# Weight pieces split ahead on POOL, and gate projections moved, in a two-block kernel of one core

## The chip, the core and the metric

The kernel runs on one core of a Trainium2 chip. Its engines are named here as the profile names them: PE multiplies matrices (TensorE), DVE, ACT and POOL work on vectors (VectorE, ScalarE, GpSimd), SP (SyncE) issues most of the transfers. The metric is the device time of one execution in microseconds (us), lower is better.

## What is computed

Two blocks follow each other, all in float32, on 512 tokens of width 1024. The first has two layers of mixer, cross-attention and feed-forward, each followed by a layer norm:

```python
for layer in range(2):
    x = layer_norm(alpha * x + mixer(x), ...)
    x = layer_norm(alpha * x + cross_attend(x, mem, ...), ...)
    x = layer_norm(alpha * x + conv_ffn(x, w_up, conv_w, conv_b, w_down), ...)
```

The second modulates the norm of x, projects it with one wide matrix, and runs a recurrent mixer and a banded attention beside each other:

```python
h = rms_norm(x, norm_g) * (1 + scale) + shift
proj = h @ w_in
ps = token_shift(proj[..., :D_SHIFT], mu_shift)      # r, k, v, g, and two low-rank inputs
y_r, g_r = rwkv7_mix(ps, ...)                        # 8 heads of 64, a state per head, token after token
q, ka, va, g_a = split(proj[..., D_SHIFT:], 4)
y_a = chunk_band_attention(q, ka, va, ...)           # 8 heads, a chunk of 64 sees itself and 8 before
y = concat(y_r * silu(g_r), y_a * silu(g_a))
x = x + gate * (y @ w_out)
```

## The kernel before

Activations stand with channels on the 128 partitions and the 512 tokens in the columns. Every large product is done in three: the weights and the activations are split into a high and a low part, and `mm3` (L260 to L265) issues high by high, high by low and low by high. A piece of weights is 128 output channels by 1024 inputs, 512 KB; with 512 tokens it feeds 8 x 3 = 24 products.

`piece` (L239) brings one: SP loads the raw 512 KB, ACT casts it to the high part (L229), and a subtract gives the low part (L230). That subtract runs on DVE in the first block and on POOL in the second (`None if self.extra else self.nc.gpsimd`). The tiles `w` are a ring of four, with two more (`wx`) in the first block, and the raw tiles a ring of two, with one more there.

`ffn` (L619) goes through its hidden channels in three chunks: the up products of a chunk, a gate piece and a value piece in turn, and then its down products, eight pieces. The epilogue of a value piece (`epi`, `m < NF`) multiplies by the gate and splits the hidden tile `hd`; that of a down piece (`epi_d`) adds to the residual x. After the last chunk come the last layer norm of the first block (`ln_half`, L382 to L412), the modulation (L710) and `open2`, which does the second block's first five projections, those of the list `OPEN`, and so r1 among them.

The second block (`block2`, L1285) has one line of work with waits. Four times `rwkv_pair` (L866) prepares two heads of the recurrence: decays and scaled keys on DVE, ACT and POOL, with L894 giving the input of the product `pb` (L834), L905, L914, L915 and L919 on POOL, and L921 a small copy on DVE. Then `rwkv_invert` (L991) inverts the triangular blocks: a chain of 31 steps on DVE (L1003, L1005), a store and a load, transposes (L1027), and two groups of small products (L834) with `fill(FILL[7])` ahead of them and `fill(FILL[8])` behind each. Then `rwkv_chain` goes through the states.

Everything else of the second block is background work, a list of generators in the order of the table ORDER: r are projections of the recurrence, q those of the attention's queries and keys, v its values (four pieces, and two goes through them), g the eight gates, p and a the attention's softmax and output, y the gating, o the last projection. `fill(us)` takes steps from the front of the list until their estimated time is spent, but takes none whose mile (the number ahead of it in ORDER) is above the line's own: 0 to 3 in the pairs, 4 in the inversion, 5 in the state chain. What a step of the line itself needs is pulled out by `need`. A scheduler then orders each engine's instructions by readiness within what the code fixes.

Of the kernel before, what the change touches and what calls it, by code (L numbers as in the profile page):

```python
# [8 lines left out]
F32 = mybir.dt.float32  # L9
# [6 lines left out]
P = 128  # L16
# [23 lines left out]
FILL = (1.12, 3, 1.5, 4, 2.08, 4.16, 23.8, 2.4, 2.4, 0.4, 4)  # L40
# [132 lines left out]
class Prog:  # L173
# [69 lines left out]

    def raw(self):
        self.n += 1
        if self.extra and self.n0 % 3 == 2:
            self.n0 += 1
            return self.t("rawx", [P, 1024], F32, 1)
        self.n0 += 1
        return self.keep.tile([P, 1024], F32, tag="raw", name=f"raw_{self.n}", bufs=2)  # L250

    def wtile(self):
        """The weights' ring: some of its room is there only in the first block."""
# [13 lines left out]
    def lin(self, src, ms, xs, epi, n=S, first=0, last=0):  # L267
        """The first (last) few blocks go through one half of the tokens, then through the other, for the LN
        before (after) them; epi(m, psum, tokens) gets the last ones by halves."""
# [43 lines left out]
    def flush(self):  # L313
        """The LN that is due."""
# [6 lines left out]
    def lin_tm(self, src, pieces, xs, ntok, epi):  # L321
        """out[tok tiles][128, 512 cols]: activations stationary, weights moving."""
# [20 lines left out]
    def rsqrt(self, y, t, v, eps):  # L343
        """y = (v + eps) ** -0.5: the table's value and a Newton step; eps is a column of self.eps."""
# [7 lines left out]
    # residual, then LN over the channels  # L352
# [61 lines left out]
    # mixer of layer 0  # L414
# [204 lines left out]
    def ffn(self, l, xs):  # L619
        nc = self.nc  # L620
        for c, (f0, f1) in enumerate(CHUNKS):
# [3 lines left out]
            def epi(m, ps, ts):  # L625
# [9 lines left out]
                else:  # L635
                    h = self.tmp()
                    nc.vector.tensor_tensor(out=h, in0=ps, in1=keep["g"], op=ALU.mult)
                    hs.append(self.split(self.hd(), h))

# [5 lines left out]
            def epi_d(m, ps, ts):  # L645
# [5 lines left out]
                if c == 1 and l == 0 and m == 1:  # L651
                    self.ada_end()
                if c == 2:
# [6 lines left out]
    # the modulation of the second block, gathered a piece at a time  # L660
# [23 lines left out]
    def ada_end(self):  # L684
        nc = self.nc
        # the sum over the partitions: within 32 of them by turning 32-blocks, then over the four groups
# [18 lines left out]
    def modulate(self, ts):  # L705
        """rms_norm(x) * norm_g * (1 + scale) + shift of half of the tokens."""
# [16 lines left out]
    def open2(self):  # L723
        """The second block's first products, of the first half of the tokens."""
# [48 lines left out]
    # The second block has one line of work with long waits (the states) and much other work for the tensor  # L773
    # engine: `bg` holds the latter as generators, and fill() puts some of it wherever the former waits.
# [57 lines left out]
    def mm(self, out, **kw):  # L832
        """A product on the line with the waits: it stays behind what fill() put before it."""
# [5 lines left out]
    def lin_g(self, src, m, xs, epi, ks=range(KT)):  # L839
        w = self.piece(self.a[src][m])  # L840
# [25 lines left out]
    def rwkv_pair(self, j):  # L866
        """What the chunks of heads 2j and 2j+1 need."""
# [9 lines left out]
        # kk  # L877
# [12 lines left out]
        # k'  # L890
        nc.scalar.activation(u, av, AF.Identity, bias=self.ka1[:, j : j + 1], scale=self.v("k_a_2", j))
        nc.vector.tensor_tensor(out=k, in0=k, in1=u, op=ALU.mult)
        # bonus
# [7 lines left out]
        # decays  # L901
# [20 lines left out]
        # values by token  # L922
# [20 lines left out]
        # scores within the chunks  # L943
# [25 lines left out]
        # keys by token  # L969
# [10 lines left out]
        # the part of the right sides that no state enters  # L980
# [10 lines left out]
    def rwkv_invert(self, prs):  # L991
        """(I - N)^-1 of each chunk's strictly triangular N: 32-blocks by substitution, then the block between."""
# [58 lines left out]
    def rwkv_chain(self, prs, tt):  # L1051
# [40 lines left out]
        def line(i, pr):  # L1092
            for _ in chunks(i, pr):
                yield FILL[9]
            # group norm, then the gate
# [33 lines left out]
    def att_v(self, half, xs):  # L1129
        """Values of two token tiles."""  # L1130
        self.va += [self.t("va", [P, S], F32, 4) for _ in range(2)]
        banks = [self.bank() for _ in range(2)]
        for jj in range(4):
            w = self.piece(self.a["in_va"][jj])
# [12 lines left out]
    def att_epi(self, m, ps):  # L1147
        """Queries or keys of a pair of heads, normed."""
# [15 lines left out]
    def att_probs(self, j):  # L1164
        """Softmax of a pair of heads: a tile holds a chunk's queries of one head, then of the other."""
# [60 lines left out]
    def gate_epi(self, n):  # L1226
        """silu(x) = (tanh(x / 2) + 1) * x / 2; the half comes where it is used."""
# [143 lines left out]
```

## Time and profile before

| | |
|---|---|
| median of three runs | 1854.24 us (1853.18 to 1855.95) |
| span of the profiled execution | 1854.5 us |
| PE busy | 1786.7 us, 96% |
| DVE busy | 1096.3 us, 59% |
| ACT busy | 783.0 us, 42% |
| POOL busy | 362.8 us, 20% |
| HBM read, written | 181.36 MB, 9.18 MB |

The span is that of one execution, taken by the hardware profiler; no time of that execution other than its span is recorded. Busy times of the engines lie beside each other, so they don't add up to the span. A table by stretches says more: the same engine is busy throughout in one stage and waits in another. PEclk in such a table is TensorE's granted clock, 1.0 for 2.4 GHz and 0.5 for 1.2 GHz.

### The profile page before, as it was taken

The page shows a single profiled execution, that of the slowest core. Times are in us where ns is not written, and L with a number is a line of the kernel's source. Part 1 is how long each engine was busy: PE and PEld are TensorE (multiplying, and loading weights), DVE is VectorE, ACT ScalarE, POOL GpSimd, SP SyncE. Part 2 cuts the span into 40 slices and gives each one's busy share as a digit, 9 for nine tenths or more (in the row PEclk, how much of TensorE's full clock was granted, in tenths as well). Part 3 has the DMA queues.
Part 4 walks back from the last instruction along what each step waited for, and adds up shares of the span by engine and source line. Part 5 has one row for each costly group of instructions (what it writes and reads, how often), then busy time and mean ns, then how long its engine had stood idle before and what let it go on. Part 6 is the DMA issues. An engine that isn't in the chain of part 4 may idle for free.

```text
span 1854.5 us, 26344 instructions
## 1 busy us (share of the span) xinstructions
PE 1786.7 (96%) x10476; PEld 1502.4 (81%) x10476; DVE 1096.3 (59%) x1741; ACT 783.0 (42%) x1319; POOL 362.8 (20%) x331
## 2 busy tenths in 40 slices
PE   8999998999999999999999999999998888879999
PEld 7889988888888888988998988888887766656657
DVE  5676689743463467444565764343447666975673
ACT  5444534532332356232453642232335645535561
POOL 0115014000000051000501400000015455623232
PEclk9999999999999999999999999999999999989999
DMA  8431455332322226333131242323222222222142
GB/s 279 145 103 60 132 181 188 100 102 91 102 92 91 80 64 196 112 96 100 59 104 35 69 125 92 102 92 100 88 86 73 82 75 88 89 74 81 56 160 103
DMA packets 62635, 192.25 MB, mean 104 GB/s; under 512 B 7344, under 2 KB 10032, under 8 KB 62512
## 3 DMA queue, kind: packets, MB, share of 16 engines
q1 hardware_dynamic: 54432, 172.25, 29.0%
q0 software_dynamic: 3248, 9.44, 1.5%
q10 hardware_dynamic: 4832, 8.88, 1.4%
q8 instruction: 82, 1.34, 0.3%
q14 instruction: 41, 0.34, 0.1%
HBM read 181.36 MB, written 9.18 MB: 103 GB/s over the span
## 4 chain that ended last, share of the span: by engine, by line
PE 76%; DVE 15%; ACT 3%; issue 3%; DMA 2%; POOL 0%; SPq 0%; DVEq 0%; ACTq 0%; POOLq 0%
PE ch L264 10%; PE ch L263 10%; PE ch L265 10%; PE mm L263 9%; PE mm L265 9%; PE mm L264 9%; PE pv L264 3%; PE pv L263 3%; PE pv L265 3%; PE ch L834 3%; DVE x L401 2%; DVE xh L405 1%; DVE w L230 1%; DVE x L400 1%; DVE vt L681 1%
## 5 line engine op out<-in xcount | busy, mean ns | idle before, releaser
L263 PE MATMUL mm<-xh,w 128*128 128x512 f32 (+1 forms) x704 | 266.1, 378 | 8.5 <-ACT w L229 7.5
L265 PE MATMUL mm<-xh,w 128*128 128x512 f32 (+1 forms) x704 | 258.6, 367 | 0.8 <-DVE w L230 0.8
L264 PE MATMUL mm<-xh,w 128*128 128x512 f32 (+1 forms) x704 | 259.0, 368 | 0.0
L370 POOL TENSOR_TENSOR t<-x,x 128x512 f32<-128x512 f32 x6 | 8.1, 1351 | 1011.1 <-ACT w L229 656.1
L229 ACT CAST w<-raw 128x1024 fp32r<-128x1024 f32 (+2 forms) x131 | 133.1, 1017 | 164.0 <-PE ch L265 62.9
L263 PEld LDWEIGHTS mm<-xh,w 128*128 128x128 f32 x704 | 135.6, 193 | 35.7 <-ACT w L229 7.8
L264 PE MATMUL ch<-xh,w 128*128 128x512 f32 (+1 forms) x432 | 154.1, 357 | 0.6 <-DVE xh L405 0.5
L264 PEld LDWEIGHTS mm<-xh,w 128*128 128x128 f32 x704 | 135.9, 193 | 22.9 <-issue 3.4
L263 PE MATMUL ch<-xh,w 128*128 128x512 f32 (+1 forms) x432 | 153.0, 354 | 1.3 <-ACT xh L404 1.3
L265 PE MATMUL ch<-xh,w 128*128 128x512 f32 (+1 forms) x432 | 152.7, 353 | 1.5 <-DVE w L230 1.5
L265 PEld LDWEIGHTS mm<-xh,w 128*128 128x128 f32 x704 | 135.8, 193 | 22.6 <-issue 1.1
L229 ACT CAST wx<-raw 128x1024 fp32r<-128x1024 f32 (+1 forms) x85 | 88.1, 1039 | 152.4 <-PE ch L265 71.5
L230 DVE TENSOR_TENSOR w<-rawx,w 128x1024 fp32r<-128x1024 f32 (+2 forms) x85 | 104.1, 1225 | 68.0 <-ACT w L229 67.6
L229 ACT CAST w<-rawx 128x1024 fp32r<-128x1024 f32 (+2 forms) x85 | 87.3, 1027 | 116.4 <-PE mm L265 71.0
L230 DVE TENSOR_TENSOR w<-raw,w 128x1024 fp32r<-128x1024 f32 (+2 forms) x90 | 113.0, 1257 | 37.8 <-ACT w L229 37.4
L230 DVE TENSOR_TENSOR wx<-raw,wx 128x1024 fp32r<-128x1024 f32 (+1 forms) x85 | 107.6, 1267 | 27.6 <-ACT wx L229 27.4
L230 POOL TENSOR_TENSOR w<-raw,w 128x1024 fp32r<-128x1024 f32 x41 | 100.4, 2456 | 119.0 <-ACT w L229 115.1
L263 PE MATMUL ch<-xh,wx 128*128 128x512 f32 (+1 forms) x304 | 103.5, 341 | 0.0
L265 PE MATMUL ch<-xh,wx 128*128 128x512 f32 (+1 forms) x304 | 103.0, 339 | 0.0
L264 PE MATMUL ch<-xh,wx 128*128 128x512 f32 (+1 forms) x304 | 103.0, 339 | 0.0
L263 PE MATMUL mm<-hd,w 128*128 128x256 f32 (+1 forms) x304 | 97.7, 322 | 3.6 <-ACT hd L229 3.6
L265 PE MATMUL mm<-hd,w 128*128 128x256 f32 (+1 forms) x304 | 97.9, 322 | 0.0
(484 smaller groups left out, 4498.6 us busy)
## 6 DMA issues: line engine op xcount, KB each, us to landing
raw<-in_up SPq DMA_DIRECT2D x56, 512.0 KB, 3.5
rawx<-in_up SPq DMA_DIRECT2D x32, 512.0 KB, 3.5
kt<-in_ada SPq DMA_DIRECT2D x48, 256.0 KB, 3.3
raw<-in_dn SPq DMA_DIRECT2D x24, 512.0 KB, 3.5
raw<-in_in_r SPq DMA_DIRECT2D x24, 512.0 KB, 3.5
raw<-in_c_in SPq DMA_DIRECT2D x16, 512.0 KB, 3.5
raw<-in_xo SPq DMA_DIRECT2D x12, 512.0 KB, 3.6
raw<-in_xv SPq DMA_DIRECT2D x11, 512.0 KB, 4.1
```

Source lines behind the costliest of these rows:

```text
L229: nc.scalar.copy(hi, src)
L230: (eng or nc.vector).tensor_tensor(out=lo, in0=src, in1=f32(hi), op=ALU.subtract)
L263: mm(out, lhsT=ah, rhs=bh, start=start, stop=False)
L264: mm(out, lhsT=ah, rhs=bl, start=False, stop=False)
L265: mm(out, lhsT=al, rhs=bh, start=False, stop=stop)
L370: eng.tensor_tensor(out=sz, in0=self.x[0][:, ts] if m == 1 else sz, in1=z, op=ALU.add)
L400: (nc.vector if k in DVE_SUB else nc.gpsimd).tensor_tensor(out=x, in0=x, in1=mn, op=ALU.subtract)
L401: nc.vector.scalar_tensor_tensor(out=x, in0=x, scalar=gk, in1=rs, op0=ALU.mult, op1=ALU.mult)
L405: nc.vector.scalar_tensor_tensor(out=lo, in0=x, scalar=bk, in1=f32(hi), op0=ALU.add, op1=ALU.subtract)
L681: nc.vector.scalar_tensor_tensor(out=dst, in0=raw, scalar=sc, in1=dst, op0=ALU.mult, op1=ALU.add)
L834: self.tc.keep_in_program_order(self.nc.tensor.matmul(out, **kw))
```

## The change

The table ORDER loses r1, and the gates g1 and g2 go from mile 5 to mile 4, behind g0. FILL[7] goes from 2.4 to 9 and FILL[8] from 2.4 to 4.2.

In the feed-forward stage of layer 1, `pre_begin` makes a list of 28 pieces of the second block (r, q, g and the four of v that ORDER names) and `pre_step` is called with each value piece of the up products and with each piece of the first two chunks' down products. A step starts the load of one piece through POOL's queue, after a copy of one element of the tile that has just been made; once two are under way, POOL casts and subtracts the older one and stores both parts, 1 MB, to DRAM. The tiles for it, `vt`, are two.

In the second block `ready` takes the place of `piece`: if a piece has been split ahead, SP loads its 1 MB straight into the ring `w`, and nothing is cast or subtracted. The eight pieces of w_out are still split there. The other lines of the diff take comments away.

```diff
-FILL = (1.12, 3, 1.5, 4, 2.08, 4.16, 23.8, 2.4, 2.4, 0.4, 4)
+FILL = (1.12, 3, 1.5, 4, 2.08, 4.16, 23.8, 9, 4.2, 0.4, 4)
...
-    (0, "r1"), (0, "r5"), (0, "r9"),
+    (0, "r5"), (0, "r9"),
...
-    (4, "v1"), (4, "q18"), (4, "q22"), (4, "q19"), (4, "q23"), (4, "g0"),
-    (5, "p0"), (5, "g1"), (5, "q20+a0"), (5, "p1"), (5, "q24+a1+p2"), (5, "g2"), (5, "g3"),
+    (4, "v1"), (4, "q18"), (4, "q22"), (4, "q19"), (4, "q23"), (4, "g0"), (4, "g1"), (4, "g2"),
+    (5, "p0"), (5, "q20+a0"), (5, "p1"), (5, "q24+a1+p2"), (5, "g3"),
...
+    def pre_begin(self):
+        self.prep, todo = {}, []
+        for _, ws in ORDER:
+            for w in ws.split("+"):
+                k, m = w[0], int(w[1:])
+                if k in "rq" and m not in OPEN:
+                    todo.append(("in_r", m))
+                elif k == "g":
+                    todo.append(("in_r", 12 + m) if m < 4 else ("in_ga", m - 4))
+                elif w == "v0":
+                    todo += [("in_va", i) for i in range(4)]
+        self.todo, self.due2 = todo, []
+
+    def pre_step(self, at):
+
+        nc = self.nc
+        if self.todo:
+            key = self.todo.pop(0)
+            t = self.t("vt", [P, 2, D], F32, 2)
+            nc.gpsimd.tensor_copy(t[:, 1, 0:1], at[:, 0:1])
+            nc.gpsimd.dma_start(out=t[:, 1, :], in_=self.a[key[0]][key[1]])
+            self.due2.append((key, t))
+        if len(self.due2) > 1 or not self.todo:
+            for key, t in self.due2[:1]:
+                self.due2.pop(0)
+                hi, lo = t[:, 0, :].bitcast(F32R), t[:, 1, :].bitcast(F32R)
+                nc.gpsimd.tensor_copy(hi, t[:, 1, :])
+                nc.gpsimd.tensor_tensor(out=lo, in0=t[:, 1, :], in1=t[:, 0, :], op=ALU.subtract)
+                name = f"sp_{key[0]}{key[1]}"
+                d = self.prep[key] = self.dram.tile([P, 2, D], F32, tag=name, name=name)
+                nc.gpsimd.dma_start(out=d, in_=t)
+
+    def ready(self, src, m):
+
+        if (src, m) not in self.prep:
+            return self.piece(self.a[src][m])
+        w = self.wtile()
+        self.nc.sync.dma_start(out=f32(w), in_=self.prep[src, m])
+        return w
...
@@ def ffn
+        if l == 1:
+            self.pre_begin()
...
                     hs.append(self.split(self.hd(), h))
+                    if l == 1:
+                        self.pre_step(f32(hs[-1][:, 0, :]))
...
+                if c < 2 and l == 1:
+                    self.pre_step(x)
...
@@ def lin_g (att_v, out_begin and out_end alike)
-        w = self.piece(self.a[src][m])
+        w = self.ready(src, m)
```

On POOL, between the layer norm ahead of the last feed-forward stage (L400) and the sums of the one behind it (L370), the kernel before has no work:

```order
L400 TENSOR_TENSOR x_84<-x_84,mean_9137 128x256
L400 TENSOR_TENSOR x_86<-x_86,mean_9137 128x256
L400 TENSOR_TENSOR x_87<-x_87,mean_9137 128x256
L370 TENSOR_TENSOR t_1466_11309<-x_80,x_81 128x512
L371 TENSOR_TENSOR t_1467_11310<-t_1467_11310,q_1483_11370 128x512
```

In the changed kernel, whose L441 is L400 of before, the pieces stand there; in_r are the raw weights and sp_in_r the split ones:

```order
L441 TENSOR_TENSOR x_87<-x_87,mean_9137 128x256
L264 COPY vt_9493<-hd_9490 128x1
L265 DMA vt_9493<-in_in_r 128x1024
L271 CAST vt_9493<-vt_9493 128x1024
L272 TENSOR_TENSOR vt_9493<-vt_9493 128x1024
L264 COPY vt_9506<-hd_9503 128x1
L275 DMA sp_in_r_9511<-vt_9493 128x2048
L265 DMA vt_9506<-in_in_r 128x1024
```

Each piece there is a copy, a load, a cast, a subtract and a store, all on POOL and its queue.

On POOL, from the last layer norm of the first block to the end of the first pair, before:

```order
L400 TENSOR_TENSOR x_87<-x_87,mean_11858 128x256
L230 TENSOR_TENSOR w_12232<-raw_12231,w_12232 128x1024
L230 TENSOR_TENSOR w_12303<-raw_12302,w_12303 128x1024
L230 TENSOR_TENSOR w_12355<-raw_12354,w_12355 128x1024
L230 TENSOR_TENSOR w_12470<-raw_12469,w_12470 128x1024
L905 TENSOR_TENSOR rt_12222<-rt_12224,rt_12222 128x512
L230 TENSOR_TENSOR w_12541<-raw_12540,w_12541 128x1024
L914 TENSOR_TENSOR ar_12282<-rk_12197,rt_12278 128x8x64
L919 TENSOR_TENSOR c_1597_12283<-rk_12202,rt_12224 64x8x64
L915 TENSOR_TENSOR rt_12246<-rt_12246,rt_12223 128x512
L919 TENSOR_TENSOR c_1597_12283<-rk_12202,rt_12224 64x8x64
L230 TENSOR_TENSOR w_12597<-raw_12596,w_12597 128x1024
```

The same place now (L952, L961, L966 and L962 are L905, L914, L919 and L915 of before):

```order
L441 TENSOR_TENSOR x_87<-x_87,mean_12054 128x256
L952 TENSOR_TENSOR rt_12418<-rt_12420,rt_12418 128x512
L961 TENSOR_TENSOR ar_12475<-rk_12393,rt_12471 128x8x64
L966 TENSOR_TENSOR c_1624_12476<-rk_12398,rt_12420 64x8x64
L962 TENSOR_TENSOR rt_12439<-rt_12439,rt_12419 128x512
L966 TENSOR_TENSOR c_1624_12476<-rk_12398,rt_12420 64x8x64
```

No subtract stands between the recurrence's own steps any more.

On PE, around the inversion's first group of small products (L834 with sav), before. The products of g0 write mm_13524, those of g1 mm_13863:

```order
L263 MATMUL mm_13524<-xh_11318,w_13520 128x512
L264 MATMUL mm_13524<-xh_11318,w_13520 128x512
L265 MATMUL mm_13524<-xh_11318,w_13520 128x512
L1182 MATMUL at_13747<-rk_13145,rk_13085 64x64 x2
L1182 MATMUL at_13756<-rk_13145,rk_13085 64x128 x2
L263 MATMUL mm_13863<-xh_11311,w_13859 128x512
L834 MATMUL ch_13590<-rt_13580,sav_12293 32x32
```

The same place now; mm_13720 belongs to g2, and the products of g0 and g1 stand ahead of it:

```order
L304 MATMUL mm_13720<-xh_11514,w_13718 128x512
L305 MATMUL mm_13720<-xh_11514,w_13718 128x512
L306 MATMUL mm_13720<-xh_11514,w_13718 128x512
L881 MATMUL ch_13754<-rt_13693,sav_12486 32x32 x16
L881 MATMUL ch_13754<-rt_13693,sav_12683 32x32 x16
L881 MATMUL ch_13791<-rt_13694,sav_12974 32x32 x16
```

The products of g1, but for the first, and all of g2's, which came later, now come ahead of the inversion's own.

In the first pair, behind the product `pb`, the kernel before has 26 products of pieces ahead of the scores, the changed one 7; in the fourth pair 41 stand ahead of `pb`, and now 34.

## Rows read from the trace of the kernel before

**Rows 1.** The page: its first line, and POOL's subtract of weight pieces

```profile
span 1854.5 us, 26344 instructions
...
L230 POOL TENSOR_TENSOR w<-raw,w 128x1024 fp32r<-128x1024 f32 x41 | 100.4, 2456 | 119.0 <-ACT w L229 115.1
```

**Rows 2.** Busy us (instructions) by stretch, then clock, DMA share and GB/s

```profile
1095.00:1385.00 290.00, 290.00 (x1274) 238.03 (x1273) 124.16 (x144) 88.67 (x110) 0.21 (x1) 1.00 0.29 93
1460.60:1600.10 139.50, 119.80 (x683) 87.25 (x682) 99.62 (x140) 72.59 (x102) 85.55 (x57) 0.93 0.26 79
1600.10:1675.00 74.90, 64.11 (x490) 48.22 (x489) 55.27 (x97) 29.11 (x44) 29.54 (x24) 0.91 0.29 89
1675.00:1790.00 115.00, 114.89 (x1001) 71.78 (x1002) 73.22 (x278) 66.47 (x185) 25.53 (x26) 1.00 0.29 99
```

**Rows 3.** PE's waits from 1400 us on: total us, times, longest us

```profile
PE ch L834 <- DVE rt L894: 17.8, 4, 4.9
PE at L710 <- ACT kt L408: 6.4, 3, 2.7
PE at L1157 <- ACT t L1153: 6.0, 2, 5.8
PE ch L834 <- DVE rt L1027: 3.3, 1, 3.3
```

**Rows 4.** Busy by stretch, columns as above: a layer norm, and stretches at half clock

```profile
1406.60:1413.40 6.80, 4.12 (x22) 3.60 (x22) 6.36 (x11) 5.07 (x13) 2.98 (x3) 1.00 0.27 78
1435.60:1442.40 6.80, 6.10 (x16) 5.03 (x17) 3.22 (x7) 4.27 (x11) 0.00 (x0) 0.50 0.40 135
1479.90:1483.30 3.40, 3.40 (x13) 2.24 (x12) 3.37 (x3) 0.72 (x1) 3.32 (x3) 0.51 0.00 0
1510.70:1517.50 6.80, 6.17 (x17) 4.13 (x18) 6.20 (x10) 0.72 (x1) 4.91 (x4) 0.50 0.17 14
1555.00:1561.80 6.80, 5.85 (x16) 3.85 (x17) 6.71 (x7) 0.72 (x1) 4.62 (x3) 0.50 0.12 41
1585.80:1589.20 3.40, 3.36 (x9) 1.70 (x10) 2.43 (x3) 0.52 (x1) 2.62 (x3) 0.51 0.17 70
1633.50:1640.30 6.80, 3.34 (x6) 2.01 (x7) 6.59 (x12) 3.22 (x5) 2.36 (x1) 0.50 0.00 0
1654.00:1660.80 6.80, 5.30 (x14) 3.98 (x14) 4.04 (x7) 0.63 (x1) 3.52 (x9) 0.50 0.44 125
```

**Rows 5.** POOL's timeline in pair 1: start, duration (us), engine, line, operation

```profile
1503.23 2.86 POOL L230 TENSOR_TENSOR w<-raw,w 128x1024 fp32r<-128x1024 f32 x1
1506.04 1.79 POOL L914 TENSOR_TENSOR ar<-rk,rt 128x512 f32<-128x512 f32 x1
```

**Rows 6.** DVE's timeline in pair 1

```profile
1503.87 2.25 DVE L921 COPY pc<-rt 128x8 f32<-128x8 f32 x1
...
1508.31 2.96 DVE L894 SCALAR_TENSOR_TENSOR rt<-rk,vec,rk 128x512 f32<-128x512 f32 x1
```

**Rows 7.** POOL's and PE's timelines behind the last layer norm; waits in brackets

```profile
1432.88 2.54 POOL L230 TENSOR_TENSOR w<-raw,w 128x1024 fp32r<-128x1024 f32 x1 [0.86 <-ACT w L229]
...
1436.30 5.49 PE L710 MATMUL at<-kt,cst 128*128 128x256 f32 x12 [1.75 <-ACT kt L408]
```

**Rows 8.** All of L1003: ns least/median/most, first and last start, some shapes

```profile
L1003 DVE TENSOR_TENSOR rt<-c,c x31: 191/374/2514, 1609.4 to 1646.9; 128x31 f32<-128x31 f32 x2, 128x60 f32<-128x60 f32 x2, 128x87 f32<-128x87 f32 x2, 128x112 f32<-128x112 f32 x2
```

**Rows 9.** DVE's subtract, 1095 to 1385 us (busy, mean ns); POOL's next work

```profile
L230 DVE TENSOR_TENSOR w<-raw,w 128x1024 fp32r<-128x1024 f32 (+1 forms) x18 | 22.3, 1239 | 3.6 <-ACT w L229 3.5
...
1384.79 1.29 POOL L370 TENSOR_TENSOR t<-x,x 128x512 f32<-128x512 f32 x1 [327.63 <-ACT w L229]
```

**Rows 10.** Transfers: KB, us from issue to landing; and the first 46.4 us

```profile
raw<-in_in_r SPq DMA_DIRECT2D x24, 512.0 KB, 3.5
...
DMA packets 5284, 12.98 MB, mean 280 GB/s; under 512 B 576, under 2 KB 1216, under 8 KB 5281
```

More of the change, by code (lines that the diff above doesn't have):

```diff
@@ L1133, in att_v @@
         for jj in range(4):
-            w = self.piece(self.a["in_va"][jj])
+            w = self.ready("in_va", jj)
             for kk in range(2):
@@ L1257, in out_begin @@
         for m in range(NPART):
-            w, ps = self.piece(self.a["out"][m]), self.bank(("mm", "mm", "ch", "ch")[m])
+            w, ps = self.ready("out", m), self.bank(("mm", "mm", "ch", "ch")[m])
             self.part.append((w, ps))
@@ L1276, in out_end @@
             else:
-                w, ps = self.piece(self.a["out"][m]), self.bank()
+                w, ps = self.ready("out", m), self.bank()
                 for k in range(KT):
```

## The prediction

> **What bounds the kernel now.** I read the page's first lines, then tables of busy time by stretch, then PE's waits, then the timelines around the longest of them. The span is 1854.5 us, the median of the runs 1854.24, so I make the sum against 1854.5 and change nothing for the difference. PE is busy for 96% of the span. In the feed-forward stage of the second layer it is busy for all 290 us of a stretch, in which POOL ran one instruction [rows 2] (its first row); in the state chain it is busy for 114.89 of 115 us [rows 2] (its last row). What is not PE's own work lies between them, from 1430 us on: in the four pairs PE stands idle for 19.7 of 139.5 us, in the inversion for 10.8 of 74.9, and the mean clock is 0.93 and 0.91 there [rows 2] (its second and third row). Time can come from three places only: fewer products, shorter waits there, and less time at 1.2 GHz.
>
> The waits are few [rows 3]: four for DVE's L894, one in each pair, 17.8 us together; three for ACT's L408 in the layer norms; one of 5.8 at L1157 and one of 3.3 at the transposes behind L1027. Behind most of them the granted clock falls from 1.0 to 0.5, for stretches of 3.4 or 6.8 us; the seven from 1430 on are in [rows 4], with PE busy for 6.10 + 3.40 + 6.17 + 5.85 + 3.36 + 3.34 + 5.30 = 33.5 us, work that takes half of that at full clock. The wait of 2.7 us ahead of 1406.6 was not followed by such a fall, and the one of 3.3 at L1027 was [rows 3, 4].
>
> Why L894 is late shows in pair 1. POOL takes a weight piece's subtract (2.86 us) at 1503.23, so L914 starts only at 1506.04, with two L919 and L915 behind it [rows 5]; on DVE the copy L921, 128 x 8 elements, lasts 2.25 us and ends together with that subtract, and L894 lasts 2.96 beside POOL's later three [rows 6]. A DVE instruction that reads SBUF here waits until the running POOL instruction is over.
>
> **The change, part by part.**
> 1. *r1 goes.* OPEN holds 1, so `open2` computes it, and ORDER computed it once more. 24 products go, at 290 / 1274 = 0.2276 us each [rows 2] (its first row): **-5.5 us**, as PE has no slack overall.
>
> 2. *The split of 33 pieces leaves block 2.* 28 pieces (four of them used twice, so 32 splits) and r1 account for 33 of POOL's 41 subtracts of 2.456 us [rows 1]; the eight of w_out stay.
>  - The last layer norm: the subtract at 1432.88 holds DVE's L401; PE waits 1.75 us and then does L710 at half clock, 12 products in 5.49 us [rows 7]. Gone: 1.75 + 6.10 / 2 = **-4.8 us**.
>  - The pairs: of 4.5 us for a mean wait at L894 I take 2.4 away in each of three pairs, one subtract [rows 1]. In the fourth I take 0.7: fewer products stand ahead of its wait now (34 instead of 41), and DVE does L913 ahead of L894. **-7.9 us**; the ends are 0 (L914, L919 and L915 alone hold L894 as long) and 4 x 2.86 = 11.4.
>  - Their clock: waits of 2.5 us or less remain, under the 2.7 that was not followed by a fall. Of (3.40 + 6.17 + 5.85 + 3.36) / 2 = 9.4 us I keep one stretch, 1.7: **-7.7 us**.
>  - The inversion: L1003 takes 0.374 us in the median of 31, up to 2.514 [rows 8], the long ones beside subtracts that are gone now, so DVE's chain ends earlier. PE feels that at its waits alone: 5.8 at L1157 and 3.34 / 2 at half clock, **-7.5 us**; at L1027 3.3 + 5.30 / 2 less 1.0 that I leave for the transposes, **-4.9 us**. Ends: 0, if the waits move to the load of the inverted blocks behind DVE's chain, and all 13.4.
>
> 3. *g1, g2 and FILL[7], FILL[8].* No product is added; g1's and g2's 48 (10.9 us) come, g1's first few excepted, ahead of the inversion's first block products and are then missing from the state chain. Where PE stands idle in the inversion they are the filler that makes part 2's gain there possible. In the state chain PE was busy throughout with this filler [rows 2] (its last row), so up to 10.9 us may open as waits; or none, if the chain was held up by the filler itself. I take **+3**, near the low end, because the scores of attention and the later gates remain as filler. Without r1 pair 0 has 7 products instead of 26 behind `pb`: 19 x 0.2276 = 4.3 us of cover, of which I take **+3** (ends 0 and 4.3).
>
> 4. *The split moves to the FFN of layer 1.* POOL issues a 512 KB load, a cast, a subtract and a 1 MB store per piece. It has nothing else until 1384.79, after 327.63 idle us [rows 9]. The cast is not in the trace; the bounds are 1.24 (DVE's subtract of that size, [rows 9]) and 2.46 (POOL's subtract, [rows 1]). With the subtract that is 3.7 to 4.9 us per piece, some 6 to 7 with the load's 3.5 us [rows 10] partly behind the other buffer: 28 pieces are 170 to 200 us, done well ahead of 1384. What they touch is DVE, which must split the stage's own weights: 18 of 1.24 us in this stretch [rows 9], and the hand-over of hidden tiles. It is busy for 124 of 290 us [rows 2] (its first row), and the ring has six places in the first block, so a piece can be split five pieces (5 x 24 x 0.2276 = 27 us) ahead of its use; that hides holds of up to 4.9 us. Only the hand-over from the up to the down products is tight. I take **+1**; the ends are 0 and 6 (three hand-overs of 2 us).
>
> 5. *1 MB loads on SP instead of 512 KB.* A piece feeds 24 products, 5.46 us; 1 MB in that time is 192 GB/s. The first 46 us of the kernel ran at 280 GB/s in the mean [rows 10], and the ring of four lets three loads be under way. I take 0; two loads of 512 KB one after the other would be 2 x 3.5 = 7.0 us, which is the last rival's price.
>
> Sum: -5.5 - 4.8 - 7.9 - 7.7 - 7.5 - 4.9 + 3 + 3 + 1 = **-31.3**, and 1854.5 - 31.3 = **1823 us**.
>
> **The skill against the trace.** The holds in [rows 6] and [rows 8] show only that DVE waits for POOL. The Trainium skill, page "SBUF — State Buffer", section "Who interferes with whom", says more: DVE instructions with two inputs in SBUF and POOL instructions that read SBUF share one pair of ports, and whichever began first holds it for its whole duration, the other fully blocking. L921's 2.25 us and L1003's 2.51 agree. That rule speaks against part 4: the lock is not removed but moved to where PE has no slack. Where the ring hides it, part 4 costs the 1 us of the sum; where it doesn't, the price is the second rival's.
>
> **Rivals.**
> - *The pairs keep their waits* (chance 0.18). L914, L919 and L915 still run beside L894, and PE reaches its wait earlier, since each pair has the same products ahead of it. Then 7.9 + 7.7 = 15.6 us stay: **1839 us**. For it: L894's 2.96 us are spent beside those three, not beside the subtract. Against it: L914 started the moment the subtract ended [rows 5].
> - *The lock reaches PE in the FFN* (0.08). In the down products a step comes with every piece: POOL's 4.9 us and DVE's own 1.24 [rows 9] exclude each other, 6.14 us where PE takes 5.46. If PE pays that for all 16 pieces, 16 x 0.68 = 11 us, and 6 for the hand-overs instead of the 1 in the sum: 1823 + 16 = **1839 us**. Against it: the ring's places, and POOL's steps, which can fall behind at no cost until 1384.79.
> - *The loads of 1 MB are late, slower than before* (0.06). With one load under way at a time a piece needs 7.0 us where PE takes 5.46: 32 x 1.54 = 49 us more, **1872 us**. It decides where a load takes over 5.46 us and the ring's next slot comes free only when the piece before is used up. Against it: 280 GB/s early on, and 79 to 89 GB/s in these stretches now [rows 2].
> - *The change doesn't split ahead*: its code order shows POOL's rows in the FFN and none of the pieces left in the pairs, so I give it nothing.
> - *The state chain misses its filler* in full: 10.9 instead of 3, **1831 us** (inside the forecast's bounds).
>
> **How the numbers follow.** Forecast 0.68, with its own bounds from 1811 to 1831: below, 3.5 more at L894 (11.4 instead of 7.9), no loss in the chain, pair 0 and the hand-overs (3 + 3 + 1) and the kept clock of 1.7, 12 in all; above, the full price of the chain's filler. The first rival has 0.18 and the second 0.08, both at 1839; the range ends 5 above them, at 1844. Left out are the late loads (0.06) and what overshoots both ends. About 0.2% (3.7 us) is what a measurement of this kernel can tell from no change. Faster takes the forecast, the first rival and nearly all of the second: 0.90; same 0.04, slower 0.06.
>
> **What would show it.** Right: 24 fewer products; POOL busy in the FFN from 1100 us and done before 1384, with PE at 100% still; no subtract on POOL from 1430 to 1675; L894's waits at 2.5 us or less with the granted clock at 1.0 behind most of them; no L1003 over 1 us; no wait at L1157. Wrong: PE waits for a `w` tile of DVE in the down products; waits for SP's loads of 1 MB in the pairs; waits at L894 as long as before; or new waits of the state chain beyond 3 us.

## The result: 1826.7 us, a ratio of 0.985

| | before | changed |
|---|---|---|
| median of four runs | 1854.95 us | 1826.68 us (1826.36 to 1828.36) |
| ratio of the two | | 0.9848, 95% interval 0.9835 to 0.9862 |
| span of the profiled execution | 1854.5 us | 1825.1 us |
| PE busy | 1786.7 us | 1772.2 us |
| POOL busy | 362.8 us | 429.2 us |
| HBM read, written | 181.36, 9.18 MB | 212.30, 38.54 MB |

The forecast was 1823 us, 3.7 us below what was measured. That the sum came so close is luck in part: several of its terms did not come out, and their errors made up for each other.

### The profile page after: what moved, and what is told of

Read it like the earlier page. It is cut to its first block, busy times and chain, and to the rows that moved or that the text cites. A ratio compares the mean times of both kernels' runs of the same rounds, so it can differ in the third digit from the quotient of the medians.

```text
span 1825.1 us, 26401 instructions
## 1 busy us (share of the span) xinstructions
PE 1772.2 (97%) x10452; PEld 1493.4 (82%) x10452; DVE 1097.2 (60%) x1739; ACT 750.9 (41%) x1285; POOL 429.2 (24%) x438
## 3 DMA queue, kind: packets, MB, share of 16 engines
HBM read 212.30 MB, written 38.54 MB: 137 GB/s over the span
## 4 chain that ended last, share of the span: by engine, by line
PE 80%; DVE 12%; ACT 3%; issue 2%; DMA 2%; POOL 0%; SPq 0%; DVEq 0%; ACTq 0%; POOLq 0%
PE ch L305 11%; PE ch L304 10%; PE ch L306 10%; PE mm L304 10%; PE mm L306 9%; PE mm L305 9%; PE pv L305 4%; PE pv L304 3%; PE pv L306 3%; PE ch L881 3%; DVE x L442 1%; DVE xh L446 1%; DVE w L230 1%; DVE x L441 1%; PE at L1229 1%
## 5 line engine op out<-in xcount | busy, mean ns | idle before, releaser
L304 PE MATMUL mm<-xh,w 128*128 128x512 f32 (+1 forms) x696 | 259.0, 372 | 9.5 <-ACT w L229 6.4
L306 PE MATMUL mm<-xh,w 128*128 128x512 f32 (+1 forms) x696 | 254.2, 365 | 0.8 <-DVE w L230 0.8
L305 PE MATMUL mm<-xh,w 128*128 128x512 f32 (+1 forms) x696 | 253.6, 364 | 0.0
L304 PEld LDWEIGHTS mm<-xh,w 128*128 128x128 f32 x696 | 132.4, 190 | 35.2 <-issue 8.6
L229 ACT CAST w<-raw 128x1024 fp32r<-128x1024 f32 (+2 forms) x98 | 98.7, 1008 | 144.1 <-PE ch L306 62.6
L306 PEld LDWEIGHTS mm<-xh,w 128*128 128x128 f32 x696 | 132.4, 190 | 22.7 <-issue 1.6
L305 PEld LDWEIGHTS mm<-xh,w 128*128 128x128 f32 x696 | 132.4, 190 | 22.3 <-issue 2.9
L230 DVE TENSOR_TENSOR w<-raw,w 128x1024 fp32r<-128x1024 f32 (+2 forms) x90 | 121.0, 1346 | 36.7 <-ACT w L229 36.3
L230 DVE TENSOR_TENSOR wx<-raw,wx 128x1024 fp32r<-128x1024 f32 (+1 forms) x85 | 114.4, 1348 | 31.0 <-ACT wx L229 30.8
L304 PE MATMUL mm<-hd,w 128*128 128x256 f32 (+1 forms) x304 | 97.7, 322 | 3.6 <-ACT hd L229 3.6
L306 PE MATMUL mm<-hd,w 128*128 128x256 f32 (+1 forms) x304 | 97.9, 322 | 0.0
L305 PE MATMUL mm<-hd,w 128*128 128x256 f32 (+1 forms) x304 | 97.4, 320 | 0.0
```

The costliest lines, as they stand in the source:

```text
L229: nc.scalar.copy(hi, src)
L230: (eng or nc.vector).tensor_tensor(out=lo, in0=src, in1=f32(hi), op=ALU.subtract)
L304: mm(out, lhsT=ah, rhs=bh, start=start, stop=False)
L305: mm(out, lhsT=ah, rhs=bl, start=False, stop=False)
L306: mm(out, lhsT=al, rhs=bh, start=False, stop=stop)
```

## The profile after

The stretches of [rows 2], each shifted to where its work lies now (busy us and instructions by engine PE, PEld, DVE, ACT, POOL, then clock, DMA share, GB/s):

```profile
1092.60:1382.60 290.00, 290.00 (x1274) 238.04 (x1273) 154.58 (x144) 88.80 (x110) 138.00 (x131) 1.00 0.68 237
1454.20:1578.00 123.80, 112.95 (x671) 83.11 (x671) 88.58 (x140) 58.05 (x87) 42.16 (x41) 0.96 0.41 146
1578.00:1644.70 66.70, 60.72 (x487) 47.52 (x486) 41.17 (x104) 21.48 (x38) 7.84 (x15) 0.95 0.62 213
1644.70:1760.70 116.00, 116.00 (x1002) 72.43 (x1001) 72.82 (x275) 62.01 (x176) 12.03 (x19) 1.00 0.28 96
```

The feed-forward stage holds the same 1274 products in the same 290.00 us, although POOL now works there for 138 us and the same 144 DVE instructions take 154.58 us instead of 124.16. The pairs are 15.7 us shorter, the inversion 8.2; the state chain is as long as before (116 us with 1002 products, against 115 with 1001).

PE's waits from 1400 us on, to be read beside [rows 3]; L881 with L941 is L834 with L894 of before, L757 is L710:

```profile
PE ch L881 <- DVE rt L941: 10.1, 4, 2.9
PE at L757 <- ACT kt L449: 5.4, 2, 2.7
PE pv L1252 <- DVE rt L1261: 3.6, 2, 3.2
PE mm L304 <- issue: 3.1, 1, 3.1
PE ch L881 <- issue: 2.9, 1, 2.9
```

17.8 us at L894 have become 10.1, the wait of 5.8 at L1157, a product in the norm of the attention's queries and keys, and that of 3.3 at L1027 are gone. Three are new or longer: 3.2 us in the last stage, and two in the inversion for which the profile names no releaser.

The stretches at half clock, beside [rows 4]:

```profile
1470.10:1473.50 3.40, 3.31 (x9) 1.68 (x10) 2.99 (x3) 0.33 (x1) 1.06 (x1) 0.50 0.41 171
1497.40:1500.80 3.40, 3.40 (x13) 2.19 (x12) 3.30 (x7) 0.72 (x1) 1.05 (x2) 0.50 0.00 0
1565.60:1569.00 3.40, 3.40 (x22) 2.93 (x22) 3.28 (x8) 1.69 (x3) 0.61 (x1) 0.51 0.17 19
1637.30:1644.10 6.80, 6.02 (x93) 5.16 (x93) 1.68 (x9) 3.55 (x9) 0.54 (x1) 0.50 0.02 6
1773.90:1780.70 6.80, 5.67 (x17) 3.12 (x18) 6.70 (x12) 0.62 (x1) 0.00 (x0) 0.50 0.59 182
```

Five instead of seven, with 21.8 us of PE's work in them instead of 33.5. The one behind the layer norm is gone; three are still there in the pairs, and the last, behind the wait of 3.2 us at L1252, is new.

In pair 1, POOL and then DVE, beside [rows 5] and [rows 6]:

```profile
1493.36 1.58 POOL L966 TENSOR_TENSOR c<-rk,rt 64x512 f32<-64x512 f32 x1 [0.77 <-DVE rk L939]
1494.90 1.25 POOL L962 TENSOR_TENSOR rt<-rt,rt 128x512 f32<-128x512 f32 x1
...
1491.36 1.26 DVE L968 COPY pc<-rt 128x8 f32<-128x8 f32 x1
...
1493.74 2.96 DVE L941 SCALAR_TENSOR_TENSOR rt<-rk,vec,rk 128x512 f32<-128x512 f32 x1
```

The subtract is gone and the copy of 8 columns takes 1.26 us instead of 2.25. L941 still takes 2.96: it is issued while POOL does L966, and it ends 0.55 us after L962, the next one, has ended.

## The experiments

### The parts of the change, one at a time

`b_r1` is the kernel before without r1 in ORDER:

```diff
-    (0, "r1"), (0, "r5"), (0, "r9"),
+    (0, "r5"), (0, "r9"),
```

> The kernel before, with r1 taken out of ORDER and nothing else changed. Theory (PE has no slack overall, so each product that goes is worth its issue time): 24 x 0.2276 = 5.5 us less, about 1849.5. Rival (r1 was filler of pair 0, and without it the waits there get longer): 0 to 2.5 us less, 1852.5 to 1855, with longer waits of PE in the first pair.

Measured: 1849.49 us, a ratio of 0.9958 (0.9941 to 0.9974) to the kernel before, 1855.92 in the same runs: 6.4 us less, with 5.5 inside the interval. PE's waits in the pairs stay as they were.

`a_order` is the changed kernel without the split ahead:

```diff
-            self.pre_begin()
+            self.prep = {}
...
-                        self.pre_step(f32(hs[-1][:, 0, :]))
...
-                    self.pre_step(x)
```

> The changed kernel without the split ahead: new ORDER and FILL, every piece of block 2 loaded raw and split on POOL as before. Theory (the split carries the gain): only r1's 5.5 us and at most 3 from the gates' places, 1846 to 1850; L894's counterpart L941 waits some 18 us in all as before and half clock returns behind it. Rival (the gates in the inversion's waits carry it): 1840 or less.

Measured: 1847.89 us, 0.9963 (0.9939 to 0.9987), the same as r1 alone. The waits of the pairs are back at full length:

```profile
PE ch L877 <- DVE rt L937: 18.2, 4, 5.3
PE at L753 <- ACT kt L449: 6.4, 3, 2.7
```

`a_oldfill` is the changed kernel with the gates and the two numbers as before:

```diff
-FILL = (1.12, 3, 1.5, 4, 2.08, 4.16, 23.8, 9, 4.2, 0.4, 4)
+FILL = (1.12, 3, 1.5, 4, 2.08, 4.16, 23.8, 2.4, 2.4, 0.4, 4)
...
-    (4, "v1"), ... (4, "g0"), (4, "g1"), (4, "g2"),
-    (5, "p0"), (5, "q20+a0"), (5, "p1"), (5, "q24+a1+p2"), (5, "g3"),
+    (4, "v1"), ... (4, "g0"),
+    (5, "p0"), (5, "g1"), (5, "q20+a0"), (5, "p1"), (5, "q24+a1+p2"), (5, "g2"), (5, "g3"),
```

> The changed kernel with g1, g2 and FILL[7], FILL[8] as before: r1 gone and the split ahead alone. Theory (the inversion's stage holds about as many projection products in both traces, 228 and 233, so the moved gates bring little): 1825 to 1830, level with the changed kernel's 1826.7. Rival (the gates fill the waits that the inversion leaves): those waits and their half clock come back, 7.5 us, 1834.

Measured: 1827.19 us, 0.9841 (0.9825 to 0.9858); the changed kernel has 0.9848 (0.9835 to 0.9862). So the moved gates and the larger fill amounts are worth nothing that can be measured, neither with the split ahead nor without it (`a_order` against `b_r1`); the intervals are 3 to 5 us to either side. With the fill as before, the inversion has one wait of 6.3 us at the transposes in place of the two of 3.1 and 2.9. The whole gain is r1's 6.4 us and some 22 of the split ahead (1849.49 - 1827.19 = 22.3; 1847.89 - 1826.68 = 21.2).

### Why PE waits in the inversion now

The changed kernel's own trace, POOL, SP, DVE and PE in turn. dt<-c stores the inverted blocks, c<-dt loads them for the transposes L1074, w<-sp_in_r is a 1 MB load of split weights, and L815 is the first step of gate g0's epilogue:

```profile
1610.64 0.55 POOL L1054 DMA_DIRECT2D dt<-c  x1 [33.10 <-DVE c L1052]
1617.91 1.61 POOL L1062 DMA_DIRECT2D c<-dt  x2 [6.71 <-DMA dt<-c]
...
1610.24 0.32 SPq L282 DMA_DIRECT2D w<-sp_in_r  x1
...
1623.02 1.29 DVE L1074 STREAM_TRANSPOSE rt<-c 32x512 f32<-32x512 f32 x2 [6.42 <-DMA c<-dt]
1624.25 0.70 DVE L815 SCALAR_TENSOR_TENSOR t<-mm,mu,t 128x511 f32<-128x511 f32 x1
...
1625.18 0.47 PE L304 MATMUL mm<-xh,w 128*128 128x512 f32 x1 [3.10 <-issue]
```

And the kernel before, POOL, at the same place:

```profile
1647.57 0.59 POOL L1007 DMA_DIRECT2D dt<-c  x1 [7.29 <-DVE c L1005]
1651.09 1.85 POOL L1015 DMA_DIRECT2D c<-dt  x2 [2.93 <-DMA dt<-c]
```

The store of 512 KB took 2.93 us and takes 6.71; from the store's issue to the transposes it is 12.4 us instead of 7.1. DVE stands 6.42 us before the transposes, with the gate's epilogue behind them in its queue; the products of g2 need the PSUM bank that this epilogue reads, so PE waits 3.10 us (read from the code, as the profile names no releaser). `a_hold` keeps the next four weight loads back until the blocks are there:

```diff
-    def ready(self, src, m):
+    def ready(self, src, m, after=None):
...
+        if (src, m) in self.early:
+            return self.early.pop((src, m))
         w = self.wtile()
+        if after is not None:
+            self.nc.gpsimd.tensor_copy(w[0:1, 0, 0:1], after[0:1, 0:1])
...
         self.fill(FILL[7])
+        for key in (("in_r", 20), ("in_r", 24), ("in_r", 15), ("in_ga", 0)):
+            self.early[key] = self.ready(*key, td)
```

> The changed kernel, in which the four 1 MB loads that come next during the inversion's store and load (q20, q24, g3, g4) wait until the inverted blocks have landed. Theory (these loads take the bandwidth, so the store and load of the blocks take 12.4 us instead of 7.1, DVE stands before its transposes, the gate's epilogue stands behind them, and PE waits 3.1 us for the bank): store and load 7 to 8.5 us, the 3.1 us wait under 1, 1821 to 1824. Rival (the loads are slow for another reason, or the gain is taken back by PE's wait for q20's weights, which now come later): round trip 11 us or more, or a new wait of 3 us or more at the first products of q20, 1826 to 1830.

Measured: 1827.26 us, 0.9847 (0.982 to 0.9874), no gain by the median; the interval is 5 us to either side. POOL's queue first, then PE's waits from 1560 to 1660 us:

```profile
1614.51 0.55 POOL L1058 DMA_DIRECT2D dt<-c  x1 [33.09 <-DVE c L1056]
1618.00 1.61 POOL L1066 DMA_DIRECT2D c<-dt  x2 [2.94 <-DMA dt<-c]
...
PE ch L885 <- issue: 2.8, 1, 2.8
PE ch L885 <- DVE rt L945: 2.6, 1, 2.6
PE at L1235 <- DVE sm L1238: 2.4, 1, 2.4
```

The store is back at 2.94 us and the wait of 3.1 is gone, so the loads did slow the store. In this trace what it brought went again into a new wait of 2.4 us of the attention (L1235) a little later, with 10.2 us at half clock there instead of 6.8. The mechanism was right; the forecast gain of 3 to 6 us did not show in the median.

### What holds L941

`a_dvekeys` takes POOL's three key instructions per pair to DVE, where they queue behind L941:

```diff
-        nc.gpsimd.tensor_tensor(out=kk, in0=kk, in1=av, op=ALU.mult)
+        nc.vector.tensor_tensor(out=kk, in0=kk, in1=av, op=ALU.mult)
...
-            nc.gpsimd.tensor_tensor(out=bk[hs, :, 1 - hh, :], in0=ch(k)[hs], in1=ch(c)[hs], op=ALU.mult)
+            nc.vector.tensor_tensor(out=bk[hs, :, 1 - hh, :], in0=ch(k)[hs], in1=ch(c)[hs], op=ALU.mult)
```

> The changed kernel with POOL's three instructions behind L961 in each pair (L962 and the two L966, 1.25 to 1.6 us each) done on DVE instead. Theory (what is left of the waits at L941, 10.1 us in four, and the half clock behind three of them, is DVE standing behind those POOL instructions: L941 lasts 2.96 us where 0.7 would do): L941 under 1 us, its four waits 2 us or less in all, half clock gone from the pairs; 8 to 12 us less, 1815 to 1819. Rival (the wait is only moved: DVE has 3 us more to do per pair and the scores behind it come later): the waits at L941 go but PE waits as long for the keys, 1825 to 1830.

Measured: 1812.84 us, 0.9768 (0.975 to 0.9786), 14 us below the changed kernel. All of L941 (least, median and most ns), PE's waits for it, and the stretch of the pairs, which holds 30 products more here than in the changed kernel's table:

```profile
L941 DVE SCALAR_TENSOR_TENSOR rt<-rk,vec,rk x4: 735/738/743, 1469.7 to 1554.8; 128x512 f32<-128x512 f32 x4
...
PE ch L881 <- DVE rt L941: 0.9, 2, 0.5
...
1454.20:1570.00 115.80, 112.96 (x701) 83.76 (x700) 84.15 (x155) 59.21 (x89) 24.13 (x28) 1.00 0.49 172
```

L941 goes from 2.98 to 0.74 us, its waits from 10.1 to 0.9, and no half clock is left in the pairs. That is the first rival's mechanism: not the subtract alone but the POOL instructions behind it held L941. By the traces the pairs' waits and half clock account for 9.2 + 5.1 = 14.3 us, but other places moved too. The wait of 3.1 us for g2's bank went, for a reason beside the edit: the store of the blocks now goes out 0.87 us ahead of the next 1 MB load, and is over in 3.21 us. The last stage's wait of 3.2 us went as well, while 10.2 us at half clock follow the stop in the inversion instead of 6.8.

```profile
1606.06 0.55 POOL L1054 DMA_DIRECT2D dt<-c  x1 [34.03 <-DVE c L1052]
1609.81 1.61 POOL L1062 DMA_DIRECT2D c<-dt  x2 [3.21 <-DMA dt<-c]
...
1606.93 0.32 SPq L282 DMA_DIRECT2D w<-sp_in_r  x1
```

### The last stage

`a_outdve` puts w_out's eight subtracts on DVE:

```diff
-        return self.split(w, raw[:, :cols], cols, None if self.extra else self.nc.gpsimd)
+        return self.split(w, raw[:, :cols], cols, None)
```

> The changed kernel with the eight subtracts of w_out, the last that POOL does in block 2, on DVE. Theory (in the last stage L1159 on DVE lasts 4.94 us behind two of them, and the copy L1261 behind it makes PE wait 3.2 us, with half clock for 6.8 us after): that wait and its half clock go, 3 to 6 us less, 1821 to 1824. Rival (DVE's 8 x 1.24 us more work delays its epilogues as much): 1826 to 1829.

Measured: 1823.15 us, 0.9818 (0.9798 to 0.9837), 3.5 us below the changed kernel; its interval and that one's (0.9835 to 0.9862) just touch, so the size of this gain is uncertain. L1159 in the changed kernel, then in this one:

```profile
L1159 DVE TENSOR_TENSOR yy<-yy,sav x4: 684/692/4943, 1752.9 to 1779.5; 128x512 f32<-128x512 f32 x4
```

```profile
L1159 DVE TENSOR_TENSOR yy<-yy,sav x4: 681/684/691, 1757.6 to 1779.3; 128x512 f32<-128x512 f32 x4
```

The wait of 3.2 us behind it and its half clock are gone.

### How much room the split ahead has

`a_out36` splits w_out's eight pieces ahead too:

```diff
+        todo += [("out", i) for i in range(8)]
         self.todo, self.due2 = todo, []
```

> The changed kernel with the eight pieces of w_out split ahead too, 36 pieces instead of 28. Theory (POOL takes 11 us per piece, since the copy that waits for a tile's store stands ahead of the next cast in its queue, and the 28 end only 8 us before POOL's sums for the layer norm): eight more pieces end some 80 us too late and hold the layer norm behind the feed-forward stage, 1890 to 1910. Rival (the pace was set by the steps' places, with slack in POOL): at most a few us late, 1820 to 1835.

Measured: 1887.64 us in one run, 32 us slower than the kernel before. The layer norm behind the feed-forward stage waits for POOL's sums:

```profile
PE at L430 <- POOL t L412: 55.1, 2, 54.9
```

In the changed kernel POOL's last store and its first sum stand like this:

```profile
1374.02 0.57 POOL L275 DMA_DIRECT2D sp_in_ga<-vt  x1 [0.30 <-POOL vt L272]
1382.50 2.06 POOL L411 TENSOR_TENSOR t<-x,x 128x512 f32<-128x512 f32 x1 [7.91 <-ACT w L229]
```

The 28 pieces begin at 1069.83, and POOL is through with them 8 us before it is needed: the change has used up all the room there is. The overrun was 55 us where 11 us per piece would give 80, so the last eight went at some 8 us each.

### Together, and what did not add up

`a_combo` has both DVE edits, and the gates and fill as before; `c_both` has both and the gates where the change put them; `c_g3` also moves g3 to mile 4; `c_split` is `c_g3` without the fill behind the first group, so that the filler stands in the second; `c_f45` is `c_both` with FILL[7] at 4.5.

> Three things at once on the changed kernel: g1, g2, FILL[7] and FILL[8] as before the change, POOL's three key instructions per pair on DVE, and the subtracts of w_out on DVE. Theory (the gains of the two DVE edits add up, and the fill as before costs nothing): 1812 to 1817. Rival (DVE, 50 to 70% busy in these stages, becomes the bound): 1823 or more.

Measured: 1819.36 us, 0.981 (0.9781 to 0.9839). The waits are short but for one of 7.0 at the transposes, and then the clock is at half for 20.5 us of the state chain with PE busy all the while:

```profile
1708.10:1728.60 20.50, 20.50 (x145) 12.81 (x144) 9.36 (x34) 6.21 (x23) 4.82 (x9) 0.50 0.42 145
```

> The changed kernel with both DVE edits (POOL's three key instructions per pair, and the subtracts of w_out), and the gates where the change put them. Theory (the two gains add up, 14 and 3.5 us; what made the version with the gates as before slower than the first edit alone was its wait at the transposes and 20 us at half clock in the state chain): 1808 to 1811. Rival (the second edit adds to DVE in a stage that the first has made tighter): 1812 to 1816.

Measured: 1811.96 us, 0.9772 (0.9747 to 0.9797), level with `a_dvekeys`: the 3.5 us of the second edit don't come on top. In `a_dvekeys` the wait of 3.2 us in the last stage was already gone.

```diff
-    (4, "v1"), ... (4, "g1"), (4, "g2"),
-    (5, "p0"), (5, "q20+a0"), (5, "p1"), (5, "q24+a1+p2"), (5, "g3"),
+    (4, "v1"), ... (4, "g1"), (4, "g2"), (4, "g3"),
+    (5, "p0"), (5, "q20+a0"), (5, "p1"), (5, "q24+a1+p2"),
```

> As c_both, with g3 too among the gates of mile 4, so that 12 products stand between the two halves of the inversion's first group of small products. Theory (more filler shortens the waits after the transposes, and PE's stop of 3 us in the second group, in which it waits for no semaphore, comes from 256 small products in a row): 1804 to 1808. Rival (the state chain pays for g3's products): 1811 or more, with waits of 1 us and more in the chain.

Measured: 1812.62 us, 0.9769 (0.9753 to 0.9786). The stop in the second group is gone, but g2 waits 7.3 us for its bank: the store of the blocks falls behind a 1 MB load again and takes 7.0 us.

> As c_g3, with the 12 products in the second group instead of the first (9 of them halfway through it). It asks where PE's stop comes from. Theory (PE's instructions run out: small products follow each other every 0.017 us, and a transfer of 16 KB of instructions ends inside the stop): with 12 long products halfway the stop is under 1.5 us or gone. Rival (PE waits for data of the loads that run then, which the profile does not name): the stop stays at 2.5 to 3 us wherever the products stand.

Measured: 1811.93 us, 0.9766 (0.9745 to 0.9786). No stop in the second group, and g2's wait for its bank is 6.9 us. PE had stood still shortly before the second group in both, so neither decides where the stop comes from.

> As c_both, with FILL[7] at 4.5 instead of 9, so that 9 of g2's products stand between the two halves of the inversion's first group of small products and no other gate is moved. Theory (PE's stop of 3.1 us in the second group is its instructions running out after some 200 small products in a row): the stop goes without any long wait ahead of it, and with it some of the 10 us at half clock behind it, 1805 to 1809. Rival (the stop went in the two versions with g3 because PE had just stood still for 7 us): the stop stays at 2.5 us or more, or a wait for the transposes of the same size takes its place, 1811 to 1814.

Measured: 1814.19 us, 0.9769 (0.9753 to 0.9786). No stop, but the rival's other half came true: 6.9 us of waits for the transposes in its place. POOL's queue shows the store at 7.05 us, and SP's that it went out 0.1 us behind a load (the second of the two in the row is issued at its end, 1611.5):

```profile
1611.59 0.55 POOL L1054 DMA_DIRECT2D dt<-c  x1 [35.04 <-DVE c L1052]
1619.19 1.61 POOL L1062 DMA_DIRECT2D c<-dt  x2 [7.05 <-DMA dt<-c]
...
1604.94 6.84 SPq L282 DMA_DIRECT2D w<-sp_in_r  x2
```

The stop itself, in `c_both`, PE in the second group of small products:

```profile
1619.14 0.24 PE L881 MATMUL ch<-mk,rt 32*32 32x32 f32 x2
...
1620.22 0.91 PE L881 MATMUL ch<-mk,rt 32*32 32x32 f32 x45
1624.23 2.39 PE L881 MATMUL ch<-mk,rt 32*32 32x32 f32 x81 [3.10 <-issue]
```

The instructions on both sides of the stop carry no wait. It is there in six kernels (the changed one, `a_hold`, `a_dvekeys`, `a_outdve`, `a_out36`, `c_both`), in which the two groups follow each other with a few products between them, and behind the same one of PE's instructions in each. It is not in those with more products or a wait there, nor in `a_order`, which has the same order of products at this place. A transfer of 16 KB of instructions ends inside it, at 1636.8 of 1635.2 to 1638.1 us in the changed kernel. In each of the traces such transfers begin once in 254 to 258 of PE's instructions (products and weight loads) in the median. At the stop 536 to 538 had begun since the last transfer did, in all six; elsewhere it is 437 at most, and 435 in `a_order`. That speaks for PE having run out of instructions; no run here changed this alone, and it stays open.

## Why the prediction was right, and which steps were not

By terms, in us, forecast and then what the traces show, with waits counted in full and PE's work at half clock by half:

| step | forecast | measured |
|---|---|---|
| r1 | -5.5 | -6.4 alone |
| layer norm, wait and clock | -4.8 | 6.4 to 5.4 at L710, 6.10 / 2 gone: -4.1 |
| waits at L894 | -7.9 | 17.8 to 10.1: -7.7 |
| half clock in the pairs | -7.7 | 9.4 to 5.1: -4.3 |
| inversion | -12.4 | 13.4 to 9.0: -4.4 |
| state chain and pair 0, missing filler | +6 | none |
| feed-forward stage | +1 | none |
| last stage | 0 | +3.2 |
| ahead of the last layer norms | 0 | -2.4 |

The last column's terms, with r1 at 5.5, make -25.2; 2.6 more are smaller waits that went (at L971, L1144, L348), and 1.6 of the spans' 29.4 I can't place.

**Right**: r1, the layer norm, and the waits at L894. The subtract of 2.46 us was taken away three times and a little more, and the waits became shorter by as much, 2.5, 2.1, 2.4 and 0.8 us from the first pair to the fourth. The 0.7 of the fourth came out by luck. In the traces 41 products stand ahead of its wait now and 34 did before, the other way round from what is said ahead of the prediction and in it; and L941 takes 2.98 us there, where L894 took 1.63. The feed-forward stage bore the split: DVE's lock came with it, as its subtracts of weights show and those of the hidden tiles. The row of [rows 9] is one of three groups, so there are 54 of the former and not 18; they take 1.52 us in the mean now instead of 1.20, and the latter 1.39 instead of 0.69. One group of each:

```profile
L230 DVE TENSOR_TENSOR w<-raw,w 128x1024 fp32r<-128x1024 f32 (+1 forms) x18 | 30.4, 1688 | 3.3 <-ACT w L229 3.1
...
L230 DVE TENSOR_TENSOR hd<-t,hd 128x512 fp32r<-128x512 f32 x18 | 25.0, 1387 | 0.0
```

The ring hid it: 290.00 us with 1274 products in both. So the second rival's cause was there and its price not. Of the subtracts of 128 x 1024 in this stretch, the 24 with no POOL instruction beside them take 1.22 us in the mean and the 22 with one 1.93. The epilogues with a PSUM input take 0.69 and 0.75 us either way. That is where the rule of the Trainium skill, "SBUF — State Buffer", section "Who interferes with whom", that a DVE instruction with two inputs in SBUF contends with a POOL instruction that reads SBUF, was borne out: DVE 30.4 us busier with the same 144 instructions, beside POOL's 138 us. L921, which the prediction gives as a case of it, is a copy with one input, which the rule in these words doesn't cover.

**Wrong, the filler.** Part 3 read from the order that 48 products were taken out of the state chain and 19 out of pair 0. But `fill` takes whatever comes next, so other pieces moved up; the state chain holds 1002 products in 116.00 busy us, and `a_oldfill` shows no difference. This error of 6 us hid those of the other sign.

**Wrong, the clock.** Part 2 took 2.7 us as the wait that is not followed by a fall. Falls followed waits of 2.14, 2.88 and 2.61 us at L941, none followed those of 2.44 there and of 2.70 in the layer norm. In `a_hold` one followed a wait of 2.43 at the same place, and in `a_dvekeys` and `c_both` one followed the layer norm's 2.7. The size of a wait alone doesn't tell.

**Wrong, the inversion.** The waits that it named went, as it said, with L1050 (L1003 of before) at 0.426 us at most instead of 2.514:

```profile
L1050 DVE TENSOR_TENSOR rt<-c,c x31: 190/359/426, 1583.1 to 1609.9; 128x31 f32<-128x31 f32 x2, 128x60 f32<-128x60 f32 x2, 128x87 f32<-128x87 f32 x2, 128x112 f32<-128x112 f32 x2
```

What the prediction left out is that a 1 MB load also delays others. Part 5 asked only whether PE would wait for the weights, and it doesn't: they land in 5.1 us, under a piece's 5.46, so the third rival's price fell away.

```profile
w<-sp_in_r SPq DMA_DIRECT2D x20, 1024.0 KB, 5.1
```

The price came where the loads share the DMA engines with the line that everything waits for, the store and load of the blocks.

**Wrong, POOL's pace.** Part 4 gave 6 to 7 us per piece, 170 to 200 us in all. It took 309 us to the landing of the last store, 11 per piece. The cast was near the low bound (1.19 us) and the subtract near the forecast (2.65), but a tile's load of raw weights lands in 6.5 us and its store in 5.1 (medians of the 20 pieces from in_r), and the copy that waits for a store stands in POOL's queue ahead of the next piece's cast:

```profile
L272 POOL TENSOR_TENSOR vt<-vt 128x1024 fp32r<-128x1024 f32 x28 | 74.2, 2650 | 2.0
L271 POOL CAST vt<-vt 128x1024 fp32r<-128x1024 f32 x28 | 33.2, 1185 | 106.8 <-DMA vt<-in_in_r 71.6 <-DMA vt<-in_in_va 27.2 <-DMA vt<-in_in_ga 8.1
```

It cost nothing, with 8 us to spare.

**The first rival** was half of the truth. I gave the forecast its case because L914 began when the subtract ended; it didn't follow that L914's successors would let L894 through. 10.1 us and 5.1 at half clock stayed; `a_dvekeys` took nearly all of them away and was 14 us faster.

**Not forecast**: 2.4 us of the spans' difference lie ahead of the last layer norms, where the change does nothing. The wait at L710 there ends at 1409.32 before, 1406.97 after, and at 1410.60 in `a_oldfill`, which has the same work up to there as the changed kernel: it differs by execution, and it arises in the first 60 us (3.5 us by PE's 300th product). A comparison of two spans here holds such a difference.

## What to carry to other kernels

A helper engine's work that blocks another should be counted by all that it has in the queue at that moment: taking one instruction away moves the next one into its place, and it pays to look at the waiting instruction's own duration (2.96 us where 0.74 does) before one counts the gain. Work that is moved to an idle stretch needs its whole round trip counted, loads and stores included, per buffer and in the order of its queue, against the next moment that the engine is needed. And transfers that grow have a price beside their own landing: look at which small transfers of the critical line are issued at the same time.

## What the runs showed of the hardware that was not expected

The store of the blocks, 512 KB, takes 6.7 to 7.1 us in the eight traces in which it is issued 0.1 to 0.4 us behind a 1 MB load, and 2.9 to 3.2 in the six in which it is issued 0.9 to 1.0 us ahead of one or without one. The Trainium skill, "DMA: Bandwidth & Descriptors", section "Queues, rings and completion order", says that each DMA engine takes turns between the queues, a packet at a time. The direction agrees; that one microsecond in the issue decides between 3 and 7 us is this case's own.

PE's clock stayed at half for 20.5 us of uninterrupted work in the state chain of `a_combo`, behind waits of 0.8 and 0.4 us, where other kernels ran the same chain at full clock throughout. What brought it about stays open.
